# One core, a two-block transformer stack: GpSimd's tensor work outside the FFNs moves to VectorE, and a head pair's value products run in one go

## The chip, the core and the metric

The kernel runs on one core of a Trainium2 chip. The core has a matrix engine (TensorE, PE in the rows; PEld is its weight load), a vector engine (VectorE, DVE), an engine for activation functions (ScalarE, ACT), a general engine (GpSimd, POOL) and SyncE (SP), which here only issues DMAs. Each engine works through a list of its own in a fixed order, and the lists meet at semaphores. TensorE writes to PSUM, a memory of 8 banks of 128 partitions x 2 KB; everything else lies in SBUF. The metric is device time in microseconds (us), lower is better.

## The reference, cut to what matters

Two different blocks follow each other on 512 tokens of width 1024. The first holds an S5 state space branch, a gated branch, cross attention to 256 memory tokens and a SwiGLU FFN; the second is run twice (two layers), each with four branches and an FFN with a short convolution:

```python
def first_block(x, mem, ...):
    n = rms_norm(h, mix_norm_g[i])
    proj = n @ w_in[i]
    ya = s5_branch(xa, ...)                 # bidirectional scan, 512 wide
    yb = sgu_branch(zu, zv, ...)            # 8 heads, chunks of 128
    h = h + (gate_a * (ya @ w_proj_a[i]) + gate_b * (yb @ w_proj_b[i])) @ w_out[i]
    h = h + memory_cross_attention(rms_norm(h, xattn_norm_g[i]), memn, ...)
    h = h + swiglu(rms_norm(h, ffn_norm_g[i]), w_gate[i], w_up[i], w_down[i])

def second_block(x, ...):
    for l in range(DEPTH_2):                # two layers
        z = rmsnorm(x, attn_norm[l]) @ w_in[l]
        yA = forgetting_attention(...)      # 8 heads of 64, causal, a decay per key
        yB = dsa_attention(...)             # 8 heads, top-256 keys chosen by an indexer
        yC = retention(...) ; yD = sliding_window_gqa(...)   # window 128, sinks
        branch = jnp.einsum('bsnc,ncd->bsnd', jnp.stack([yA, yB, yC, yD], 2), w_branch[l])
        x = x + jnp.sum(jax.nn.sigmoid(gates) * branch, axis=2) @ w_out[l]
        a, b = jnp.split(causal_dwconv(rmsnorm(x, ffn_norm[l]) @ w_up[l], ...), 2, axis=-1)
        x = x + (jax.nn.silu(a) * b) @ w_down[l]

def forgetting_attention(...):              # the shape that yB and yD share
        p = jax.nn.softmax(jnp.where(causal, logits, neg), axis=-1)
        return jnp.einsum('bhqs,bshd->bqhd', p.astype(v.dtype), v)
```

## The kernel before, in words

Activations lie transposed, feature on partition, as 8 tiles of 128x512. A product in full precision is made of three products of rounded parts: every operand is split into a rounded part `hi` and a rest `lo`, and `mm3` (L186 to L191) multiplies hi by hi (L189), hi by lo (L190) and lo by hi (L191). So each weight tile of 128x1024 comes by DMA into `raw` (2 buffers), ScalarE rounds it into `hi` (`split`, L167), and `lo = raw - hi` is a subtraction through the helper `tt` (L112). `hi` and `lo` have 3 buffers each; a weight tile feeds 24 matmuls of 512 columns. Who subtracts is set by `weights` (L177 to L185) with a counter: `lo_every` is 1000 in the mixing parts (`mix1`, `mix2`), where GpSimd does nearly all, 2 from `memory_k` to the end of the cross attention, where GpSimd does every second one, and 0 in the FFNs, where VectorE does all. Some other elementwise work is written for GpSimd: six of eight adds of a norm's sums of squares (`square_sum`), the sine product of `rope`, the sum over branches (`merged`), two products of `retain`, one of four output products of `finish`, and the products of the FFNs.

Attention in the second block runs for pairs of heads. `attend` (L952) is a generator that the projections around it advance a step at a time (`pump`): for each of the four chunks of 128 queries the scores (into a PSUM bank `sc`), their maximum (L968), Exp, the reciprocal and the scaling (L982); one chunk later two sets of transposes (L995), ScalarE's copy of them to `probT` (L998, 3 buffers of 512), and the value products (L1003): one head fills rows 0 to 63 of the only `pv` bank, the other rows 64 to 127, so each is a matmul with 64 columns of weights, where the other matmuls around it have 128. There are 8 pairs a layer whose chunks see 1, 2, 3 and 4 key blocks (20 value products) and 4 with 1, 2, 2 and 2 (14). A value product is in float32 and shows as two matmuls in the trace. `select` finds the 256 best keys with 16 rounds of MAX8 (L1127) and MATCH_REPLACE8 (L1128) for three chunks of queries, 48 of each a layer, on VectorE.

The order on each engine is not written out: the code gives a program order, the tile framework puts every instruction into its engine's list by priority and by its own model of durations, and it gives out buffers (`g` has 52 slots of 128x512). `high_priority` pulls instructions ahead, and `manual_schedule` keeps those of one engine together in the order that is written.

## Time and profile before

| | us |
|---|---|
| median of 3 runs (3116.22 to 3117.85) | 3117.04 |
| the profiled execution, its own time | 3118.62 |
| span of the profiled execution | 3116.7 |
| TensorE busy | 3031.5 |
| VectorE busy | 1884.2 |
| ScalarE busy | 1352.9 |
| GpSimd busy | 974.6 |

The stages of the span, by when their weights are fetched: 0 to 480 us the first mixing part, to 605 the cross attention, to 962 the first FFN, 962 to 1605 and 2045 to 2715 the mixing parts of the two layers, 1605 to 2045 and 2715 to the end their FFNs. A matmul's record lasts longer than the time until the next may start, so a busy TensorE is read together with the distances between starts. In the chain of work that ended last, each step is followed back to what released it.

### The profile page before, as it was taken

What the parts mean: (1) busy time and instruction counts of PE and PEld (TensorE: products, weight loads), DVE (VectorE), ACT (ScalarE), POOL (GpSimd) and SP (SyncE); (2) the same over time, 40 slices, a digit from 0 to 9 for tenths busy, and PEclk for the clock granted to TensorE, in tenths of its full rate; (3) what the DMA queues carried; (4) which work ended last, traced back from release to release, by engine and by line L of the source; (5) the groups of instructions that cost most, each with busy time, mean ns of one, the idle gap of its engine ahead of it and who ended that gap; (6) DMA issues with size and microseconds to landing.
All of it is one profiled execution on the core that took longest, in us unless ns stands there. A gap on an engine that the chain in (4) does not pass through costs nothing.

```text
span 3116.7 us, 39233 instructions
## 1 busy us (share of the span) xinstructions
PE 3031.5 (97%) x14922; PEld 2481.6 (80%) x14922; DVE 1884.2 (60%) x3423; ACT 1352.9 (43%) x2278; POOL 974.6 (31%) x594
## 2 busy tenths in 40 slices
PE   8998999999999999999999999999999999999998
PEld 6877878888887777778888888888677778888887
DVE  7899454454455596455456665548845455465575
ACT  5523343332224475646334333356555452343343
POOL 3234243210014442345454000054333445610011
PEclk9999999999999999999999999999999999999999
DMA  5223343223333321222223323242211222333332
GB/s 161 75 80 95 102 146 105 95 88 102 101 90 94 102 75 55 68 78 82 78 88 122 95 91 105 81 133 78 68 55 61 92 75 78 122 96 100 95 96 80
DMA packets 98075, 287.10 MB, mean 92 GB/s; under 512 B 11984, under 2 KB 20432, under 8 KB 97888
## 3 DMA queue, kind: packets, MB, share of 16 engines
q1 hardware_dynamic: 97888, 284.61, 29.6%
q8 instruction: 117, 1.92, 0.3%
q14 instruction: 70, 0.57, 0.1%
HBM read 274.64 MB, written 9.93 MB: 91 GB/s over the span
## 4 chain that ended last, share of the span: by engine, by line
PE 82%; DVE 11%; ACT 2%; DMA 2%; issue 2%; POOL 1%; SPq 0%; DVEq 0%; ACTq 0%; POOLq 0%
PE psmm L189 24%; PE psmm L190 24%; PE psmm L191 24%; DVE tmp L112 3%; PE pspv L1003 2%; DVE g L112 2%; PE pssc L995 1%; DVE g L1128 1%; DVE m L1127 1%; PE pssc L1093 1%; DVE tmp L1217 1%; PE pssc L1094 1%; DVE s5t L112 0%; PE pspv L791 0%; PE pssc L759 0%
## 5 line engine op out<-in xcount | busy, mean ns | idle before, releaser
L191 PE MATMUL psmm<-g,lo 128*128 128x512 f32 (+1 forms) x3456 | 1346.8, 390 | 4.0 <-POOL lo L112 4.0
L190 PE MATMUL psmm<-g,hi 128*128 128x512 f32 (+1 forms) x3456 | 1348.2, 390 | 1.5 <-DVE g L171 1.5
L189 PE MATMUL psmm<-g,hi 128*128 128x512 f32 (+1 forms) x3456 | 1346.4, 392 | 2.3 <-ACT g L167 1.3
L167 ACT CAST hi<-raw 128x1024 fp32r<-128x1024 f32 (+3 forms) x506 | 507.6, 1005 | 1035.3 <-PE psmm L190 748.5
L112 POOL TENSOR_TENSOR lo<-raw,hi 128x1024 fp32r<-128x1024 f32 (+1 forms) x259 | 630.6, 2436 | 1008.8 <-ACT hi L167 849.2
L191 PEld LDWEIGHTS psmm<-g,lo 128*128 128x128 f32 x3456 | 650.3, 188 | 138.4 <-POOL lo L112 5.3
L189 PEld LDWEIGHTS psmm<-g,hi 128*128 128x128 f32 x3456 | 650.2, 188 | 135.4 <-ACT hi L167 3.1
L190 PEld LDWEIGHTS psmm<-g,hi 128*128 128x128 f32 x3456 | 650.8, 188 | 132.3 <-issue 2.6
L112 POOL TENSOR_TENSOR tmp<-tmp,tmp 128x512 f32<-128x512 f32 (+1 forms) x121 | 166.8, 1381 | 1019.1 <-DVE tmp L1419 570.7
L112 DVE TENSOR_TENSOR lo<-raw,hi 128x1024 fp32r<-128x1024 f32 (+2 forms) x247 | 298.0, 1207 | 90.7 <-ACT hi L167 90.6
L112 DVE TENSOR_TENSOR tmp<-psmm,g 128x512 f32<-128x512 f32 x236 | 161.4, 688 | 295.9 <-PE psmm L191 248.3
L189 PE MATMUL psmm<-hi,g 128*128 128x512 f32 (+1 forms) x384 | 144.5, 384 | 16.4 <-ACT g L124 11.1
L1445 DVE SCALAR_TENSOR_TENSOR g<-psmm,g 128x512 f32<-128x512 f32 x88 | 60.7, 690 | 151.7 <-PE psmm L191 151.7
L124 ACT ACTIVATE prob<-prob,nmx 128x128 f32<-128x128 f32 (+2 forms) x192 | 102.5, 535 | 106.7 <-DVE nmx L968 105.9
L190 PE MATMUL psmm<-lo,g 128*128 128x512 f32 (+1 forms) x384 | 146.5, 384 | 2.4 <-POOL lo L112 2.4
L191 PE MATMUL psmm<-hi,g 128*128 128x512 f32 (+1 forms) x384 | 145.2, 382 | 0.0
L112 DVE TENSOR_TENSOR g<-tmp,g 64x512 fp32r<-64x512 f32 (+1 forms) x162 | 130.5, 806 | 14.1 <-ACT g L167 11.0
L124 ACT ACTIVATE tmp<-tmp 128x512 f32<-128x512 f32 (+1 forms) x138 | 84.2, 613 | 111.4 <-DVE tmp L112 98.5
L1419 DVE SCALAR_TENSOR_TENSOR tmp<-tmp,vec,tmp 128x511 f32<-128x511 f32 (+1 forms) x176 | 131.0, 746 | 2.0 <-ACT tmp L124 0.6
L998 ACT COPY probT<-pssc 128x128 f32<-128x128 f32 (+2 forms) x192 | 69.8, 397 | 88.3 <-PE pssc L995 83.3
L189 PEld LDWEIGHTS psmm<-hi,g 128*128 128x128 f32 x384 | 75.1, 196 | 29.2 <-ACT g L124 11.1
L982 DVE TENSOR_SCALAR prob<-prob,sm 128x128 f32<-128x128 f32 (+2 forms) x192 | 93.2, 527 | 2.5
(276 smaller groups left out, 3117.6 us busy)
## 6 DMA issues: line engine op xcount, KB each, us to landing
raw<-w_up SPq DMA_DIRECT2D x110, 512.0 KB, 3.5
raw<-w_gates SPq DMA_DIRECT2D x64, 512.0 KB, 3.5
raw<-w_down SPq DMA_DIRECT2D x72, 384.0 KB, 3.1
raw<-w_rope SPq DMA_DIRECT2D x40, 512.0 KB, 3.6
raw<-w_branch SPq DMA_DIRECT2D x32, 512.0 KB, 3.5
raw<-w_out SPq DMA_DIRECT2D x24, 512.0 KB, 3.6
raw<-w_gate SPq DMA_DIRECT2D x22, 512.0 KB, 3.7
raw<-w_fox SPq DMA_DIRECT2D x16, 512.0 KB, 3.5
```

Source lines behind the costliest of these rows:

```text
L112: (eng or self.nc.vector).tensor_tensor(out, a, b, op)
L124: self.nc.scalar.activation(out, in_, func, **k)
L167: nc.scalar.copy(hi, src)
L189: mm(out, sh, mh, start=start, stop=False)
L190: mm(out, sh, ml, start=False, stop=False)
L191: mm(out, sl, mh, start=False, stop=stop)
L982: nc.vector.tensor_scalar(pt[i][:, :nk], pt[i][:, :nk], sm[:, i:i + 1], None, ALU.mult)
L995: nc.tensor.transpose(tr[:, j * P:(j + 1) * P], pt[i][:, j * P:(j + 1) * P], self.ident)
L998: nc.scalar.copy(ptT[:, :n * P], tr[:, :n * P])
L1003: nc.tensor.matmul(pv[i * 64:(i + 1) * 64, pc * P:(pc + 1) * P], value(i, b), tt[i][:, j * P:(j + 1) * P], start=j == 0, stop=j == n - 1)
L1419: nc.vector.scalar_tensor_tensor(o[:, sh:], u[:, :S - sh], w, o[:, sh:], ALU.mult, ALU.add)
L1445: self.nc.vector.scalar_tensor_tensor(self.x[d], ps, 0.5, self.x[d], ALU.mult, ALU.add)
```

## The change

All GpSimd arithmetic outside the FFNs goes to VectorE: the `lo` subtractions of all weights (with the counter and its four constants gone), the sums of squares, the sine products, the sum over branches, `retain`'s products and the output's. What stays on GpSimd are the FFNs' products, memsets and a few small copies. In `attend` a chunk's transposed probabilities are kept in buffers of their own size until the pair's last chunk; then all value products of the pair are issued together, last chunk first, in a block that is scheduled by hand and with high priority. `g` loses 4 slots.

```diff
-NSLOT = 52
+NSLOT = 48
-LO_MIX1, LO_MEM, LO_MIX2, LO_FFN = 1000, 2, 1000, 0
+NPT = (2, 6, 2, 2)
...
-        self.n_lo += 1
-        pool = self.lo_every and self.n_lo % self.lo_every != 0
-        self.split(hi[:, :width], lo[:, :width], raw[:, :width], eng=self.nc.gpsimd if pool else None)
+        self.split(hi[:, :width], lo[:, :width], raw[:, :width])
...
-            self.add(acc, acc, sq, self.nc.gpsimd if k < KT - 2 else None)
+            self.add(acc, acc, sq)
...
-            self.add(self.merged[d], self.merged[d], t, nc.gpsimd)
+            self.add(self.merged[d], self.merged[d], t)
...
-                    self.mul(o[:, i], self.x[q * 4 + i][:, ts], rb, nc.gpsimd if i == 3 else None)
+                    self.mul(o[:, i], self.x[q * 4 + i][:, ts], rb)
...
-        self.mul(xs, xs, self.sinR, nc.gpsimd)
+        self.mul(xs, xs, self.sinR)
...
-        pv = None
+        done = []
...
-                if pv is None:
-                    pv = self.bank("pv")
...
-                    ptT = self.t(self.ap, [P, S], "probT", bufs=3)
-                    nc.scalar.copy(ptT[:, :n * P], tr[:, :n * P])
+                    ptT = self.t(self.ap, [P, n * P], f"probT{n}", bufs=NPT[n - 1])
+                    nc.scalar.copy(ptT, tr[:, :n * P])
                     tt.append(ptT)
+                done.append((pc, bl, tt))
                 yield
+            pend = nxt
+
+        pv = self.bank("pv")
+        with self.tc.manual_schedule(engines={mybir.EngineType.PE}), self.tc.high_priority():
+            for pc, bl, tt in reversed(done):
                 for j, b in enumerate(bl):
                     for i in range(2):
                         nc.tensor.matmul(pv[i * 64:(i + 1) * 64, pc * P:(pc + 1) * P],
                                          value(i, b), tt[i][:, j * P:(j + 1) * P],
-                                         start=j == 0, stop=j == n - 1)
-                yield
-            pend = nxt
+                                         start=j == 0, stop=j == len(bl) - 1)
+        yield
...
-                    self.mul(qx[:, j], q[j][:, cs], xi[:, j], nc.gpsimd)
+                    self.mul(qx[:, j], q[j][:, cs], xi[:, j])
...
-                    self.mul(Rn, R, gC, nc.gpsimd)
+                    self.mul(Rn, R, gC)
...
-                self.add(self.merged[d], self.merged[d], g, nc.gpsimd)
+                self.add(self.merged[d], self.merged[d], g)
...
-        self.mul(self.cosR, self.cload("cos"), self.rb, nc.gpsimd)
-        self.mul(self.sinR, self.cload("sin"), self.rb, nc.gpsimd)
+        self.mul(self.cosR, self.cload("cos"), self.rb)
+        self.mul(self.sinR, self.cload("sin"), self.rb)
```

The list of TensorE before, in layer 0, where one head pair's chunks 1 to 3 follow each other (`pspv`, L1003 are its value products, `probT` its transposed probabilities, `h` the values of four key blocks; `pssc` of L1081, L1082, L1093 are scores and of L995 transposes of `prob`):

```order
L1081 MATMUL pssc_2034_9699<-g_1868_9005,g_1866_9003 128x512
L1082 MATMUL pssc_2034_9699<-g_1872_9009,g_1870_9007 128x512
L1003 MATMUL pspv_2011_9620<-probT_2027_9684,h_1641_8124 64x128
L1081 MATMUL pssc_2035_9703<-g_1869_9006,g_1867_9004 128x512
L1082 MATMUL pssc_2035_9703<-g_1873_9010,g_1871_9008 128x512
L1003 MATMUL pspv_2011_9620<-probT_2029_9689,h_1641_8124 64x128
L1003 MATMUL pspv_2011_9620<-probT_2027_9684,h_1642_8125 64x128
L1003 MATMUL pspv_2011_9620<-probT_2029_9689,h_1642_8125 64x128
L995 MATMUL pssc_2036_9712<-idn_2_71,prob_2020_9664 128x128 x3
L995 MATMUL pssc_2038_9718<-idn_2_71,prob_2021_9665 128x128 x3
L1003 MATMUL pspv_2011_9620<-probT_2037_9716,h_1641_8124 64x128
```

The pair's value products stand one to six at a time, with scores and transposes of 128 columns between them. The list of TensorE now, for the first head pair of layer 0 (the value products are L1000 here, and `probT4` holds chunk 3):

```order
L187 MATMUL psmm_2027_9648<-g_1572_7762,hi_2029_9651 128x512
L188 MATMUL psmm_2027_9648<-g_1571_7761,lo_2030_9652 128x512
L1000 MATMUL pspv_1804_8758<-probT4_1791_8700,h_1641_8124 64x128
L1000 MATMUL pspv_1804_8758<-probT4_1793_8707,h_1641_8124 64x128
L1000 MATMUL pspv_1804_8758<-probT4_1791_8700,h_1642_8125 64x128
L1000 MATMUL pspv_1804_8758<-probT4_1793_8707,h_1642_8125 64x128
L1000 MATMUL pspv_1804_8758<-probT4_1791_8700,h_1643_8126 64x128
L1000 MATMUL pspv_1804_8758<-probT4_1793_8707,h_1643_8126 64x128
L1000 MATMUL pspv_1804_8758<-probT4_1791_8700,h_1644_8127 64x128
L1000 MATMUL pspv_1804_8758<-probT4_1793_8707,h_1644_8127 64x128
L1000 MATMUL pspv_1804_8758<-probT3_1787_8687,h_1641_8124 64x128
L1000 MATMUL pspv_1804_8758<-probT3_1789_8693,h_1641_8124 64x128
```

The run goes on through chunks 2, 1 and 0 to 20 value products without another instruction between them. Over the whole program the value products stand in 139 groups before and in 34 now: 8 of 20, 8 of 19, 6 of 14, 2 of 13 and 10 single ones that stand a few instructions ahead of their run.

The list of VectorE before, in layer 0, amid the selection (`m8` and the `g` beside it are the 8 largest scores and the scores of one chunk; L968 are the maxima of attention scores):

```order
L112 TENSOR_TENSOR tmp_1957_9380<-tmp_1957_9380,tmp_1958_9381 128x512
L1127 MAX m8_1848_8937<-g_1715_8444 128x8
L1127 MAX m8_1874_9029<-g_1662_8254 128x8
L1127 MAX m8_1875_9032<-g_1693_8359 128x8
L112 TENSOR_TENSOR h_1598_7878<-psmm_1971_9426,g_1585_7807 128x512
L1128 MATCH_REPLACE g_1715_8444<-m8_1848_8937,g_1715_8444 128x512
L1128 MATCH_REPLACE g_1662_8254<-m8_1874_9029,g_1662_8254 128x256
L1128 MATCH_REPLACE g_1693_8359<-m8_1875_9032,g_1693_8359 128x384
L968 ISA prob_1828_8863,nmx_1829_8864<-pssc_1832_8870,cst2_1589_7837 128x128
L968 ISA nmx_1829_8864 128x1
L1127 MAX m8_1876_9035<-g_1715_8444 128x8
```

No `lo` stands between the first and the last of the layer's 48 MAX8 (they are in the list of GpSimd). The list of VectorE now, at a place of the same stretch (MAX8 is L1123, MATCH_REPLACE L1124, the helper of L112 is L111):

```order
L1123 MAX m8_1883_9061<-g_1662_8254 128x8
L1123 MAX m8_1884_9064<-g_1693_8359 128x8
L111 TENSOR_TENSOR lo_2078_9873<-raw_2076_9870,hi_2077_9872 128x1024
L111 TENSOR_TENSOR g_1819_8838<-tmp_1817_8834,g_1819_8838 64x512
L1124 MATCH_REPLACE g_1715_8444<-m8_1858_8965,g_1715_8444 128x512
L111 TENSOR_TENSOR g_1826_8845<-tmp_1818_8835,g_1822_8841 64x512
L1124 MATCH_REPLACE g_1662_8254<-m8_1883_9061,g_1662_8254 128x256
L1124 MATCH_REPLACE g_1693_8359<-m8_1884_9064,g_1693_8359 128x384
L111 TENSOR_TENSOR h_1601_7881<-psmm_2042_9735,g_1585_7807 128x512
L973 RECIPROCAL sm_1810_8789<-sm_1810_8789 128x2
L973 RECIPROCAL sm_1836_8885<-sm_1836_8885 128x2
```

Between the first and the last MAX8 of layer 0 the list of VectorE now has 235 instructions where it had 205: 19 `lo` of 1024 columns, 4 sine products of 512 columns and 7 others more. The list of TensorE has 459 matmuls of 512 columns in float32r between the same two marks where it had 394. Layer 1 reads alike (236 for 202, 19 `lo`).

## Rows read from the trace of the kernel before

**Rows 1.** The page: busy time by engine, then the chain that ended last, by engine.

```profile
PE 3031.5 (97%) x14922; PEld 2481.6 (80%) x14922; DVE 1884.2 (60%) x3423; ACT 1352.9 (43%) x2278; POOL 974.6 (31%) x594
...
PE 82%; DVE 11%; ACT 2%; DMA 2%; issue 2%; POOL 1%; SPq 0%; DVEq 0%; ACTq 0%; POOLq 0%
```

**Rows 2.** Busy time by engine in seven stretches: stretch, its us, busy us (instructions).

```profile
0.00:310.00 310.00, 279.11 (x1417) 229.95 (x1418) 265.59 (x568) 128.60 (x181) 116.19 (x89) 0.98 0.35 103
605.00:962.00 357.00, 357.00 (x1579) 295.35 (x1578) 177.41 (x199) 103.05 (x128) 36.84 (x25) 1.00 0.32 95
962.00:1058.00 96.00, 85.93 (x406) 71.84 (x405) 59.12 (x71) 53.08 (x82) 53.90 (x29) 0.93 0.36 113
1058.00:1177.00 119.00, 114.34 (x544) 90.26 (x543) 104.40 (x252) 76.74 (x140) 52.17 (x31) 1.00 0.23 74
1177.00:1605.00 428.00, 425.38 (x2295) 337.47 (x2294) 227.62 (x573) 210.59 (x458) 180.26 (x101) 1.00 0.23 73
2108.00:2230.00 122.00, 115.77 (x552) 91.72 (x550) 110.06 (x250) 77.74 (x140) 52.34 (x31) 1.00 0.24 76
2230.00:2715.00 485.00, 480.99 (x2537) 383.31 (x2536) 254.38 (x599) 232.38 (x487) 218.68 (x120) 1.00 0.25 79
```

**Rows 3.** TensorE in order of time: start us, us, one value product between matmuls.

```profile
1389.23 0.39 PE L189 MATMUL psmm<-hi,g 128*128 128x512 f32 x1
1389.55 0.43 PE L1003 MATMUL pspv<-probT,msc 128*64 128x128 f32 x2
1389.91 0.39 PE L1093 MATMUL pssc<-g,g 128*128 128x256 f32 x1
```

**Rows 4.** TensorE in order of time: plain matmuls, then eight value products in a run.

```profile
1248.10 0.39 PE L190 MATMUL psmm<-g,hi 128*128 128x512 f32 x1
1248.32 0.39 PE L191 MATMUL psmm<-g,lo 128*128 128x512 f32 x1
1248.64 1.09 PE L1003 MATMUL pspv<-probT,msc 128*64 128x128 f32 x16
1249.66 0.33 PE L1093 MATMUL pssc<-g,g 128*128 128x128 f32 x1
```

**Rows 5.** Line 1003, the value products: forms, with min/median/max ns of one.

```profile
L1003 PE MATMUL pspv<-probT,msc x544: 272/273/325, 1227.5 to 2571.7; 128*64 128x128 f32 x182
L1003 PE MATMUL pspv<-probT,h x320: 272/273/325, 1113.2 to 2278.5; 128*64 128x128 f32 x160
```

**Rows 6.** Groups of instructions, GpSimd: shapes and count | busy us, mean ns.

```profile
L112 POOL TENSOR_TENSOR lo<-raw,hi 128x1024 fp32r<-128x1024 f32 x255 | 622.8, 2444 | 990.8 <-ACT hi L167 831.2 <-PE pssc L995 53.4 <-issue 27.8
```

**Rows 7.** The same view, VectorE.

```profile
L112 DVE TENSOR_TENSOR lo<-raw,hi 128x1024 fp32r<-128x1024 f32 x159 | 216.0, 1358 | 90.6 <-ACT hi L167 90.6
L112 DVE TENSOR_TENSOR tmp<-psmm,g 128x512 f32<-128x512 f32 x236 | 161.4, 688 | 295.9 <-PE psmm L191 248.3 <-ACT tmp L925 24.3 <-ACT g L266 8.9
L112 DVE TENSOR_TENSOR s5h<-s5h,s5t 128x64 f32<-128x64 f32 x63 | 30.9, 491 | 1.8
```

**Rows 8.** GpSimd, then VectorE, in order of time around one `lo`.

```profile
1496.23 2.41 POOL L112 TENSOR_TENSOR lo<-raw,hi 128x1024 fp32r<-128x1024 f32 x1 [3.30 <-ACT hi L167]
...
1497.03 1.63 DVE L112 TENSOR_TENSOR es<-vec,nmx 128x2 f32<-128x2 f32 x1
1498.93 0.16 DVE L112 TENSOR_TENSOR sm<-sm,es 128x2 f32<-128x2 f32 x1 [0.27 <-ACT es L124]
```

**Rows 9.** Who TensorE waited for: us in total, times, longest.

```profile
PE pssc L661 <- DVE s5b L654: 4.9, 1, 4.9
PE pspv L379 <- DVE tmp L383: 4.1, 4, 1.3
PE pspv L1003 <- ACT probT L998: 4.1, 8, 0.9
PE psmm L191 <- POOL lo L112: 4.0, 3, 1.7
```

**Rows 10.** The chain in order of time: start us, us; the longest VectorE burst.

```profile
1574.83 8.13 DVE tmp L1217 x21
```

More of the change, by code (lines that the diff above doesn't have):

```diff
@@ L78, in __init__ @@
         self.bg, self.bg2 = [], []
-        self.lo_every, self.n_lo = 0, 0
         pool = lambda name, bufs, **k: ctx.enter_context(tc.tile_pool(name=name, bufs=bufs, **k))
@@ L161, in debug, with split @@
             self.nc.sync.dma_start(self.O[name], ap)
-    def split(self, hi, lo, src, scale=None, eng=None):
+    def split(self, hi, lo, src, scale=None):
         nc = self.nc
@@ L167, in split @@
             nc.scalar.copy(hi, src)
-            self.sub(lo, src, hi.bitcast(F32), eng)
+            self.sub(lo, src, hi.bitcast(F32))
         else:
@@ L303, in mix1 @@
         nc, I = self.nc, self.I
-        self.rate, self.lo_every = 1, LO_MIX1
+        self.rate = 1
         xa_d = self.dram.tile([S, 512], F32, name="xa_d")
@@ L313, in mix1 @@
                 raws[k // 2] = self.raw(I["w_xa"][k // 2], 1024)
-        self.lo_every = 0
         for u in range(4):
@@ L332, in mix1 @@
                              u == 0 and k == 0, u == 3 and k == 1)
-        self.lo_every = LO_MIX1
         for c in range(CHUNKS):
@@ L410, in mix1 @@
                 rm = fin()
-        self.lo_every = LO_MEM
         self.memory_k(m, rm[0])
@@ L800, in ffn1 @@
         nc, I = self.nc, self.I
-        self.lo_every = LO_FFN
         x, fin = self.rms_prep(self.x, "g_ffn", S)
@@ L1303, in mix2 @@
         nc, ap, I = self.nc, self.ap, self.I
-        self.rate, self.lo_every = 1, LO_MIX2
+        self.rate = 1
         wr = I["w_rope"][l]
@@ L1400, in ffn2 @@
         cw, cb = self.vec(f"cw{l}"), self.vec(f"cb{l}")
-        self.lo_every = LO_FFN
         j = 0
```

## The prediction

> **What bounds the kernel now.** I read the page first. TensorE is busy 3031.5 of 3116.7 us, and the chain that ended last lies on it for 82% and on VectorE for 11% [rows 1]. A busy share is an average, so the busy time by stretch comes next [rows 2]: in the first FFN TensorE is busy for all of 357 us, and in the later parts of the two mixing stages (1177 to 1605, 2230 to 2715) for over 99%. The first 310 us (279 of 310) and the head of layer 0 (86 of 96) are the loose ones. In three stretches VectorE is nearly full: the first 310 us (266 busy) and the two selections (104 of 119, 110 of 122). GpSimd is full nowhere. So a gain has to come from time on TensorE that does no work although it counts as busy, or from waits in the loose stretches; a loss would come through VectorE where it is full. For the first, the order of time on TensorE shows distances between starts [rows 3, 4]; for the second, the groups on GpSimd and VectorE and a place where the two meet [rows 6 to 8]; who TensorE waited for closes the list [rows 9].
>
> **The value products.** A plain matmul of 512 columns starts 0.22 us after the one before [rows 4]; over all pairs of them the median is 0.227. A value product after such a matmul starts 0.32 us after it, and the next full-width matmul starts 0.36 us after a lone product [rows 3]. Beyond the plain 0.227 the lone product costs 0.32 + 0.36 - 0.227 = 0.45 us. Eight in a run take 0.32 + 1.02 = 1.34 us, less 0.227 = 1.11 [rows 4]. The two heads of a pair write different halves of the array and start within 6 ns of each other when they alternate, so eight products are eight steps (four pairs, two records each) where the lone one is two: (1.11 - 0.45) / 6 = 0.11 us a step, and 0.45 - 0.22 = 0.23 us are fixed, paid for the change from 128 to 64 columns and back. A lone product takes the time of two.
>
> There are 864 records, 432 products [rows 5], and before they stand in 139 groups. By size: 67 of one or two products at 0.45, 40 of three or four at 0.68, 8 of five at 0.89, 8 of six at 1.2, 16 of seven or eight at 1.11: 30 + 27 + 7 + 10 + 18 = 92 us; a count of the single groups in the trace gives 93.9, and I use that. Now there are 34: 16 of 19 or 20 products, 20 steps each, 0.23 + 2.20 = 2.43; 8 of 13 or 14, 1.77; 10 lone ones, 0.45: 39 + 14 + 4.5 = 57.6. The gain is 36 us. Fourteen of the old groups lie in the selections, where VectorE may set the pace; I leave their share, 4 us, out. **-32 us** (bounds -36 and -15; the lower end is in the rivals). The other 32 lie where TensorE is busy over 99% [rows 2], so they are on the path. What is late next there: the runs need the last chunk's transposes copied by ScalarE, which is busy about half of those stretches [rows 2].
>
> **GpSimd's work on VectorE.** GpSimd made 255 `lo` of 1024 columns at 2.44 us [rows 6]. VectorE's own take 1.36 in the mean [rows 7], and 1.225 is the median of the 133 that have no GpSimd instruction beside them. With some 130 products and sums of 512 columns at 0.69 (the mean of a VectorE product of that size [rows 7]), 24 small ones and the rest, VectorE takes on 414 us of instructions. Against this stands what GpSimd costs it now. An instruction of 2 elements lasted 1.63 us and ended with the `lo` on GpSimd (1497.03 + 1.63 = 1498.66, 1496.23 + 2.41 = 1498.64), and its like right after, with GpSimd idle, 0.16 [rows 8]. An add of 64 columns in the S5 scan has a mean of 0.49 [rows 7] where its median alone is 0.225. Products that read PSUM show no such stretching: 0.688 [rows 7] for all, 0.691 alone. Taking each VectorE instruction against the median of its own kind without GpSimd beside it, 312 us of VectorE's time are such waiting, 43 of them in FFN stretches, where GpSimd stays. So VectorE ends near 1884 + 414 - 269 = 2029 us, 65% of the span. From 1177 to 1605 it gets 94 more and 49 back on 228 of 428: that is hidden behind TensorE, and free. Where VectorE is full it has to be counted.
>
> *Selections.* In layer 0 the list of VectorE between the first and the last MAX8 gains 19 `lo` (23.3 us), 4 sine products (2.7) and 7 small ones (2.6), 28.6 in all, and gets 10 back: 104.4 + 28.6 - 10 = 123 us busy, and with today's 14.6 us of waits 138. The list of TensorE between the same marks takes 65 matmuls (14.8) and 14 transposes (1.5) more, so 119 + 16 = 135 would be no loss. Between 123 and 138 against 135, twice: -20 to +6; the waits stay where they are in part, and I take **+2 us** for both.
>
> *First 310 us.* VectorE takes over 39 `lo` and 10 sums, 53 us, and gets 75 back. TensorE's waits on VectorE and GpSimd in the first 480 us are 18.5 us, the largest among them 4.9 on a small S5 copy and 4.1 on the gate's sum [rows 9]. A third of these is my estimate, **-6 us**, between -18 and +10 (an S5 chain that now shares its queue with the `lo`).
>
> *Heads of the layers.* From 962 to 1058 TensorE idles 10 us [rows 2] behind norms whose adds of 512 columns GpSimd did and VectorE now does at 0.69 [rows 7]; VectorE takes on 24 us there and gets 23 back. **-4 us** with the smaller head of layer 1, between -8 and +2.
>
> *Queues.* A `lo` now waits behind whatever VectorE is at; behind it waits TensorE's third matmul of each step. With three buffers of `hi` and `lo`, and 24 x 0.227 = 5.4 us of matmuls a weight tile, a `lo` may come some 5 us late before TensorE sees it. The output's one product and the four slots less of `g` I put at 0, between -1 and +3: nothing but TensorE's look-ahead hangs on the slots, and its list shows the selections reaching further ahead than before.
>
> **Sum.** The profiled execution took 3118.62 us: -32 + 2 - 6 - 4 gives 3078.6. That execution lies 1.6 above the median of the runs, so I predict **3077 us**, 40 less.
>
> **A rule that speaks against it.** The rows just named show VectorE waiting out GpSimd. The Trainium skill, Perfetto Trace Analysis, section Optimizing Scalar/DVE Operations, says that when the vector engine is saturated, moving some of its work to ScalarE or even GpSimd may make sense, and adds that between these two it might not help, since they share a read port. By its first half this change goes the wrong way in the three full stretches, and the sum would be that of rival 1, 3119; the trace bears out its second half, 1.63 us for 0.16 [rows 8].
>
> **The rivals.**
> 1. *VectorE fills up.* If its instructions do not get shorter, the selections need 104.4 + 28.6 + 14.6 = 148 us against 135, +12 each, and the first stretch 266 + 53 = 319 of 310, +10: -32 + 24 + 10 and no gain at the heads, 3118.6 + 2 - 1.6 = 3119: no change. For it: VectorE's 104 of 119 us in the selection [rows 2]. Against it: the stretching in rows 7 and 8, which cannot outlive its cause.
> 2. *Late `lo`, the slower end.* If VectorE falls more than one weight tile behind, each of the 39 + 19 + 19 = 77 `lo` in the full stretches can hold TensorE for the instruction ahead of it, 0.69 us: +53, so 3077 + 53 = 3130; with half of the selections of rival 1, 24 / 2 = 12 more, 3142. I price it at 3136, between them. It decides from a backlog of 5.4 us on; one burst in the trace is longer, 8.1 us [rows 10], with few `lo` beside it. Against it: GpSimd's `lo` of 2.44 us cost TensorE's third matmuls only 4.0 us in three waits [rows 9].
> 3. *The runs wait.* Each of 24 runs may wait for its last copy. Such waits now are 4.1 us in 8, the longest 0.9 [rows 9]; 24 x 0.9 = 22 us takes two thirds of the gain: 3099. It is also what the change gives if the runs do not hold together on the chip as in the list.
> 4. *More comes back.* If VectorE's shorter instructions remove all 18.5 us of waits in the first 480 us and the selections end 8 us earlier, 3077 - 12.5 - 8 = 3057.
>
> **How the numbers follow.** Forecast 0.62 (3064 to 3090), rival 1 0.07, rival 2 0.06, rival 3 0.13, rival 4 0.12. The range takes in the forecast, rivals 3 and 4 and leaves out 0.13: 3055 to 3105. A difference of 0.2% (6.2 us) is about what a measurement tells from none: faster 0.62 + 0.13 + 0.12 = 0.87, same 0.07, slower 0.06.
>
> **What would show it.** The runs: line 1000 with 0.11 us a step and 105 groups fewer, so 1177 to 1605 shortens by 15 us and 2230 to 2715 likewise. VectorE: `lo` at 1.23, the 2-element adds at 0.16, total near 2030. The selections (first to last MAX8): 135 us, with 459 matmuls in them. Waits of TensorE on `lo` near 0. Wrong would be: selections of 145 us or more (rival 1), TensorE waiting on `lo` in VectorE's name by tens of us (rival 2), line 1000 waiting for `probT4` by a microsecond each (rival 3).

## The result and the profile after

The changed kernel takes 3062.94 us (median of 4 runs, 3062.15 to 3063.27) beside 3116.89 us for the kernel before (4 runs): a ratio of 0.9826 (0.9809 to 0.9843), 54 us less. I had predicted 3077, 40 less, with a range of 3055 to 3105. The direction and the range held; where the time came from did not, as the marks below show.

The page of the changed kernel, busy time by engine and the chain that ended last (beside [rows 1]); its profiled execution took 3062.15 us:

```profile
PE 2985.7 (98%) x14922; PEld 2486.8 (81%) x14922; DVE 1983.2 (65%) x3869; ACT 1353.1 (44%) x2276; POOL 116.6 (4%) x148
...
PE 89%; DVE 7%; ACT 2%; DMA 1%; issue 1%; SPq 0%; DVEq 0%; ACTq 0%
```

TensorE is busy 46 us less with the same 14922 matmuls. VectorE is busy 99 us more, where the forecast had 145. That is not a smaller load: the forecast added up lengths of records, and busy time counts records that overlap only once. Added up in the same way, VectorE's records went from 2035 to 2175 us, 140 more.

To see where, I use three marks that both programs pass in the same order: the first product of the gate in each of the three FFNs (the span from the first to the last is 283.7 us in the first FFN and 286.4 or 286.3 in the others, in both kernels, so nothing happened inside them). One line before, then after; each row gives the first and the last start:

```profile
L816 DVE SCALAR_TENSOR_TENSOR tmp<-tmp,tmp x22: 679/684/692, 639.6 to 923.3; 128x512 f32<-128x512 f32 x22
L1424 DVE SCALAR_TENSOR_TENSOR tmp<-tmp,tmp x22: 676/684/692, 1706.9 to 1993.2; 128x512 f32<-128x512 f32 x22
L1424 DVE SCALAR_TENSOR_TENSOR tmp<-tmp,tmp x22: 680/684/686, 2761.4 to 3047.8; 128x512 f32<-128x512 f32 x22
```

```profile
L809 DVE SCALAR_TENSOR_TENSOR tmp<-tmp,tmp x22: 679/685/692, 610.7 to 894.4; 128x512 f32<-128x512 f32 x22
L1419 DVE SCALAR_TENSOR_TENSOR tmp<-tmp,tmp x22: 678/684/687, 1664.9 to 1951.3; 128x512 f32<-128x512 f32 x22
L1419 DVE SCALAR_TENSOR_TENSOR tmp<-tmp,tmp x22: 680/685/687, 2706.2 to 2992.5; 128x512 f32<-128x512 f32 x22
```

The first FFN begins 28.9 us earlier; layer 0 (from the first mark to the second) takes 1054.2 instead of 1067.3, 13.1 less; layer 1 takes 1041.3 instead of 1054.5, 13.2 less. So more than half came from the first block, to which the forecast gave 6, and 26 from the two layers, to which it gave 34.

Busy time in stretches of the changed kernel (columns as in [rows 2]: stretch, its us, then busy us and instructions of TensorE, its weight load, VectorE, ScalarE and GpSimd, then TensorE's granted clock):

```profile
0.00:282.00 282.00, 271.09 (x1418) 227.59 (x1419) 234.85 (x612) 125.23 (x175) 12.08 (x40) 1.00 0.37 111
934.00:1018.00 84.00, 81.22 (x407) 68.82 (x406) 59.22 (x99) 52.78 (x82) 3.60 (x8) 0.98 0.40 131
1017.00:1148.00 131.00, 125.80 (x595) 102.35 (x594) 120.41 (x282) 80.69 (x146) 2.08 (x4) 0.99 0.24 77
1150.00:1190.00 40.00, 30.97 (x209) 25.18 (x210) 23.95 (x77) 24.05 (x65) 0.00 (x0) 0.83 0.04 14
```

The first 1417 matmuls took 310 us before, and 1418 take 282 now. The head of layer 0, 406 matmuls before and 407 now, shrank from 96 to 84 us. The selection holds 595 matmuls in 131 us where it held 544 in 119: the same pace. And right behind it is a stretch that the forecast did not have: 40 us in which TensorE is busy for 31 and is granted 0.83 of its clock.

Who TensorE waited for (us in total, times, longest; beside [rows 9]):

```profile
PE pssc L986 <- DVE prob L975: 23.1, 10, 4.3
...
PE psmm L188 <- DVE lo L111: 3.5, 4, 0.9
...
PE pspv L1000 <- ACT probT L989: 0.7, 2, 0.3
```

The late `lo` that rival 2 feared cost 3.5 us. The runs' own wait for their last copy, which rival 3 priced at 22 us, is 0.7 us. But the transposes of the probabilities (L986) now wait 23.1 us for VectorE to scale them (L975).

### The profile page after: what moved, and what is told of

Same layout as the page of the kernel before. It is cut to its first block, busy times and chain, and to the rows that moved or that the text cites. A ratio compares the mean times of both kernels' runs of the same rounds, so it can differ in the third digit from the quotient of the medians.

```text
span 3060.3 us, 38946 instructions
## 1 busy us (share of the span) xinstructions
PE 2985.7 (98%) x14922; PEld 2486.8 (81%) x14922; DVE 1983.2 (65%) x3869; ACT 1353.1 (44%) x2276; POOL 116.6 (4%) x148
## 4 chain that ended last, share of the span: by engine, by line
PE 89%; DVE 7%; ACT 2%; DMA 1%; issue 1%; SPq 0%; DVEq 0%; ACTq 0%
PE psmm L186 26%; PE psmm L188 26%; PE psmm L187 26%; PE pspv L1000 2%; PE pssc L986 1%; DVE g L111 1%; DVE lo L111 1%; DVE g L1124 1%; DVE m L1123 1%; DVE tmp L111 1%; DVE prob L961 1%; PE pssc L1089 1%; PE pssc L1090 0%; PE pspv L785 0%; PE pssc L753 0%
## 5 line engine op out<-in xcount | busy, mean ns | idle before, releaser
L111 DVE TENSOR_TENSOR lo<-raw,hi 128x1024 fp32r<-128x1024 f32 (+3 forms) x506 | 610.7, 1207 | 215.7 <-ACT hi L166 214.2
L111 DVE TENSOR_TENSOR tmp<-psmm,g 128x512 f32<-128x512 f32 x236 | 161.8, 689 | 294.2 <-PE psmm L188 274.4
L186 PE MATMUL psmm<-hi,g 128*128 128x512 f32 (+1 forms) x384 | 142.7, 380 | 13.5 <-ACT g L123 10.8
L111 POOL TENSOR_TENSOR tmp<-tmp,tmp 128x512 f32<-128x512 f32 x66 | 89.7, 1360 | 1535.2 <-DVE tmp L1414 979.4
L111 DVE TENSOR_TENSOR g<-tmp,g 64x512 fp32r<-64x512 f32 (+2 forms) x166 | 113.4, 684 | 18.1 <-ACT g L166 11.0
L986 PE MATMUL pssc<-idn,prob 128*128 128x128 f32 x432 | 71.2, 286 | 24.1 <-DVE prob L975 23.1
L186 PEld LDWEIGHTS psmm<-hi,g 128*128 128x128 f32 x384 | 73.7, 192 | 25.6 <-ACT g L123 10.8
L918 ACT COPY tmp<-psmm 32x512 f32<-32x512 f32 x160 | 92.5, 578 | 2.4
```

Source lines behind the costliest of these rows:

```text
L111: (eng or self.nc.vector).tensor_tensor(out, a, b, op)
L186: mm(out, sh, mh, start=start, stop=False)
L918: nc.scalar.copy(xs[k * 32:k * 32 + 32], bk[(k ^ 1) * 32:(k ^ 1) * 32 + 32])
L986: nc.tensor.transpose(tr[:, j * P:(j + 1) * P], pt[i][:, j * P:(j + 1) * P], self.ident)
```

## The experiments

In the table each kernel's marks are read on the same two lines as above: by how much the first FFN begins earlier (-) or later than in the kernel before, and by how much each layer is shorter (-) or longer. The median of before, measured beside each batch, was 3117.85 for e1 to e4, 3117.2 for e5 to e8 and 3116.8 for e9 to e12.

| kernel | median us | ratio to before (95%) | first FFN | layer 0 | layer 1 |
|---|---|---|---|---|---|
| changed | 3062.9 | 0.9826 (0.9809-0.9843) | -28.9 | -13.1 | -13.2 |
| e1 runs only | 3140.4 | 1.0073 (1.0058-1.0088) | +0.4 | +11.9 | +7.2 |
| e2 move only | 3072.0 | 0.9856 (0.9840-0.9873) | -27.7 | -10.7 | -7.4 |
| e3 move, first block | 3094.9 | 0.9924 (0.9909-0.9939) | -26.3 | +4.5 | -2.4 |
| e4 lo twice | 3124.5 | 1.0021 (1.0012-1.0030) | +33.4 | -12.7 | -11.3 |
| e5 norm adds | 3114.4 | 0.9992 (0.9982-1.0002) | -4.6 | +1.9 | -0.2 |
| e6 2 steps | 3049.8 | 0.9783 (0.9769-0.9798) | -28.6 | -21.8 | -17.2 |
| e7 scores first | 3068.5 | 0.9841 (0.9826-0.9856) | -30.1 | -11.1 | -6.9 |
| e8 one more step | 3059.7 | 0.9816 (0.9801-0.9830) | -32.3 | -13.4 | -13.3 |
| e9 move only, 2 steps | 3073.5 | 0.9858 (0.9842-0.9874) | -27.1 | -7.5 | -7.7 |
| e10 lead | 3048.1 | 0.9781 (0.9767-0.9796) | -31.3 | -20.6 | -17.7 |
| e11 head by head | 3093.0 | 0.9924 (0.9909-0.9939) | -31.1 | +2.3 | +7.2 |
| e12 lo in selection | 3042.5 | 0.9762 (0.9747-0.9776) | -28.4 | -21.6 | -19.7 |

### The two parts apart: e1 and e2

e1 puts the new `attend` (with NSLOT 48 and NPT) into the kernel before; e2 puts the old one (with NSLOT 52) into the changed kernel.

```diff
 # e1, against the kernel before
-NSLOT = 52
+NSLOT = 48
+NPT = (2, 6, 2, 2)
...
+                done.append((pc, bl, tt))
...
+            for pc, bl, tt in reversed(done):
```

> The kernel before with the new attend alone (value products in runs, buffers by size, 48 slots of g); GpSimd keeps all its work. Theory: a value product's group costs 0.23 us plus 0.109 us a step, so 105 groups fewer give back 32 to 36 us wherever GpSimd's work is done, and nothing else moves: 3117 - 33 = 3084 us (3079 to 3090), with the waits of TensorE in the selections as before (about 4 us each layer). Rival: the 10 us a layer that the changed kernel lost to waits of the transposes on the scaled probabilities come from the runs, which leave nothing but one pair's softmax to work on: then this kernel has them too, 3084 + 20 = 3104 us.

> The changed kernel with the attend of before (value products chunk by chunk, 52 slots): only GpSimd's work is moved to VectorE. Theory: the first 605 us give back 29 us, the heads of the layers 12 and 1, and VectorE's 19 further lo in each selection cost 10 us a layer: 3117 - 42 + 20 = 3095 us (3088 to 3102). Rival (the waits in the selections belong to the runs): 3117 - 42 = 3075 us. By my prediction's own terms (+2 - 6 - 4) it would be 3109 us.

The runs alone made the kernel 22 us slower, worse than the rival of e1, and the move alone made it 46 us faster, near the rival of e2 (3075). The four slots less of `g` and the new `probT` buffers go with the runs in both kernels and were not tried apart. The waits of TensorE in e1 and then in the kernel before, the spans and mean granted clocks of the two, and the same 100 us of each by windows:

```profile
PE pssc L994 <- DVE prob L983: 31.3, 21, 3.0
PE pssc L994 <- DVE nmx L969: 10.8, 5, 3.0
```

```profile
PE pssc L995 <- DVE prob L982: 6.0, 5, 2.2
...
PE pssc L995 <- DVE nmx L968: 2.8, 4, 1.7
```

```profile
core 0: 3137.4 us, clock 0.982
```

```profile
core 0: 3116.7 us, clock 0.991
```

```profile
1150.00:1250.00 100.00, 86.12 (x465) 70.37 (x464) 75.16 (x181) 60.76 (x137) 23.78 (x11) 0.90 0.15 48
```

```profile
1150.00:1250.00 100.00, 95.65 (x550) 73.01 (x549) 70.21 (x188) 56.97 (x135) 26.39 (x11) 1.00 0.18 55
```

The transposes wait 42.1 us in 26 places (31.3 on the scaling, 10.8 on the maximum); in the kernel before it was 8.8 us in 9. Around such waits TensorE is granted its lower level, 1.2 GHz, for a while (0.90 in the mean of these 100 us of e1, 1.00 in those of before). Over the span the mean of 0.982 leaves out 0.018 x 3137 = 56 us, where the kernel before, with a mean of 0.991, leaves out 28. The account: -36 for the groups (the forecast's own price), +33 for the waits, +28 for the clock, -4 for the waits on `probT` that are gone: +21. The span grew by 20.7.

The waits of e2 show the other side, with the transposes' waits where they were, and its mean clock:

```profile
PE pssc L987 <- DVE prob L974: 7.7, 3, 4.3
```

```profile
core 0: 3068.9 us, clock 0.995
```

### What is late, seen in the changed kernel

TensorE, then VectorE, then ScalarE, in order of time, in the stretch behind the first selection (start us, us, what, count, and in brackets the idle time ahead):

```profile
1162.29 1.03 PE L986 MATMUL pssc<-idn,prob 128*128 128x128 f32 x6
1167.57 1.97 PE L986 MATMUL pssc<-idn,prob 128*128 128x128 f32 x8 [4.25 <-DVE prob L975]
...
1171.56 3.19 PE L1000 MATMUL pspv<-probT,h 128*64 128x128 f32 x38
```

```profile
1163.24 0.08 DVE L961 DVE_READ_ACCUMULATOR2_ANT nmx<- 128x1 f32 x1
1163.35 2.84 DVE L111 TENSOR_TENSOR g<-tmp,g 64x512 fp32r<-64x512 f32 x4
1166.82 0.17 DVE L973 RECIPROCAL sm<-sm 128x2 f32<-128x2 f32 x1 [0.63 <-ACT prob L123]
1167.02 0.88 DVE L975 TENSOR_SCALAR prob<-prob,sm 128x512 f32<-128x512 f32 x2
```

```profile
1161.83 2.55 ACT L929 CAST g<-tmp 64x512 fp32r<-64x512 f32 x4
1164.40 0.48 ACT L989 COPY probT<-pssc 128x384 f32<-128x384 f32 x1
1164.90 0.72 ACT L123 ACTIVATE prob<-prob,nmx 128x512 f32<-128x512 f32 x1
...
1165.62 0.46 ACT L989 COPY probT<-pssc 128x384 f32<-128x384 f32 x1
1165.98 0.72 ACT L123 ACTIVATE prob<-prob,nmx 128x512 f32<-128x512 f32 x1
```

The last scores of the chunk end near 1162.3. The way from there through the maximum, the exponential, the reciprocal and the scaling takes until 1167.5, five microseconds, and TensorE's list holds six transposes of 0.11 us for that time. It idles 4.25 us, and the run of 19 products behind it begins at the lower clock (0.53 granted from 1166.0 to 1172.8): 38 records in 3.19 us, where 40 take 2.40 at full clock (below). VectorE is named because its scaling is the last step, but the longest stay is on ScalarE: both maxima are read by 1163.3, and the two exponentials begin at 1164.90 and 1165.98, behind four casts and two copies. So ScalarE's order made this wait, too; another order was not tried.

In the list of the kernel before, 1.1 us of value products of earlier chunks and 1.4 us of a projection stood in this place besides; in e2 it was 0.5 us of value products alone, and there the transposes did not wait. Counting TensorE's work in the lists between a head's last score of a chunk and the first transpose of it, with the trace's distances (0.227 us for 512 columns, 0.119 for 256, 0.109 for 128), 18 of the 192 sets of transposes have less than 4 us of it in the kernel before, 24 in e2, 40 in e1 and 53 in the changed kernel. So the theory became: the runs save what they promise, and the order that comes with them takes away what covered the softmax.

What went is for the smaller part the value products themselves. The 29 sets that fall below 4 us from e2 to the changed kernel lose 3.8 us of projections each in the mean and 0.1 us of value products (in some a run of the pair before stands there now): the order of the list changed around them. And less cover is not all of it. In the changed kernel every wait of the transposes lies at a set with less than 4 us of work, but in e1 31 of the 42 us lie at sets with 6 to 21 us, where the way to the scaled probabilities took 7 to 24 us. What made it so long beside GpSimd's work was not tried.

### Testing the cover: e6, e9, e8, e7, e10

e6 changes one number of the changed kernel, e9 the same number of e2; e8 adds a step; e10 is e6 with other leads; e7 is e6 with `with self.tc.high_priority():` around the scores and around the softmax in `attend`.

```diff
 # e6 and e9, in mix2
-        self.rate = 4
+        self.rate = 2
 # e8, in attend
                 done.append((pc, bl, tt))
                 yield
+                yield
 # e10, beside rate = 2
-LEAD = (4, 3, 3, 3)
+LEAD = (4, 4, 3, 4)
```

> The changed kernel with one number changed: in the first half of a layer's mixing part a projection advances the attention by 2 steps instead of 4. In TensorE's list 40 instead of 53 of the 192 sets of transposes then stand less than 4 us of TensorE's work behind their scores, the runs stay whole (34 groups). Theory (TensorE waits because the runs took away what lay between a chunk's scores and its transposes): the 23 us of waits of the transposes on the scaled probabilities fall to 12 to 17, and the time to 3048 to 3058 us. Rival (VectorE is full in the selections, whatever the order): waits as before, 3060 us or more.

> The kernel with the move alone (value products chunk by chunk as before) and 2 steps a projection instead of 4 in the first half of a layer's mixing part, the number that made the changed kernel 13 us faster. Its list of TensorE has 27 sets of transposes less than 4 us behind their scores where it had 24. Theory (2 steps help only because they give the runs' transposes back what lay between them and their scores): no gain, 3068 to 3078 us beside 3072. Rival (2 steps are better for any order of the value products): about 3060 us, and the runs are worth no more than before.

One row each, the transposes' wait on the scaling in e6 and in e9:

```profile
PE pssc L986 <- DVE prob L975: 15.5, 8, 3.4
```

```profile
PE pssc L987 <- DVE prob L974: 6.9, 6, 4.4
```

e6 gave 3049.8 us and 15.5 us of waits, both inside what the theory said; with the value products spread as before, the same number gave nothing (3073.5 beside 3072.0). So the 13 us belong to the order with runs. Compared like with like the runs are worth 3073.5 - 3049.8 = 24 us with 2 steps, 9 us with 4 (3072.0 - 3062.9) and a loss of 22 beside GpSimd's work.

> The changed kernel with one more step for each chunk of the attention, which the attend of before has (its value products were a step of their own): 47 instead of 53 sets of transposes stand less than 4 us behind their scores, 36 groups of value products. Theory: a part of the waits goes, 5 to 10 us: 3053 to 3060 us. Rival (the steps have nothing to do with it): 3063 us, with the 23 us of waits as they are.

> The changed kernel with 2 steps (3050 us) and with one more gate projection ahead of two of the four branch products, so that other work stands between the last pairs' softmax steps: 34 instead of 40 sets of transposes less than 4 us behind their scores, 36 groups. Theory: 3 to 8 us less, 3042 to 3047 us. Rival (what is left of the waits is VectorE's): 3048 to 3052 us.

e8 took 3 us off, at 3059.7 inside its range, with 19.4 us of waits, but it proves little: its layers are as long as the changed kernel's (it waits 4 us less, and its mean clock of 0.988 leaves out 9 us more), and its gain lies ahead of the first FFN, where the lists of the two kernels are the same. (In e6 and e10 they are the same there too, and the marks of these four lie between -28.6 and -32.3: so far apart can single executions be.) e10 came to 3048.1, which is the rival's side: the waits went from 15.5 to 13.4 us and the time by less than can be told apart.

> The same with the scores and the softmax of the attention scheduled at high priority: 30 of the 192 sets of transposes stand less than 4 us behind their scores, but scores now cut the runs into 93 groups, 59 more, each at 0.23 us: +13.6 us. Theory: the waits of the transposes fall to 6 to 12 us, which gives 11 to 17 us and the half clock that goes with them, about 5: 3063 + 14 - 19 = 3058 us (3050 to 3065). If the groups cost nothing beyond their steps: 3044 us. If the waits stay: 3077 us.

e7 had 11.0 us of such waits, as expected, and still took 3068.5, slower than its range. By the distances between starts its 93 groups cost 79 us, the 34 of e6 62: 17 more where 59 x 0.23 = 14 were counted. TensorE is busy 25 us more (3009.2 instead of 2983.8); where the other 8 come from I did not separate. Two thirds of the 93 begin behind a score of 256 columns. Here, cover bought by cutting the runs cost more than it gave.

Among these kernels, which all have the runs and VectorE's `lo`, the waits on the scaling follow the count of short sets: 53, 47, 40, 34 and 30 sets (changed, e8, e6, e10, e7) and 23.1, 19.4, 15.5, 13.4 and 11.0 us.

### The price of a step: e11

```diff
-            for pc, bl, tt in reversed(done):
-                for j, b in enumerate(bl):
-                    for i in range(2):
+            for i in range(2):
+                for pc, bl, tt in reversed(done):
+                    for j, b in enumerate(bl):
```

> The changed kernel, in which a run goes through the products of the first head and then through those of the second, so that neighbours no longer write different halves of the array. Still 34 groups. Theory (two heads that alternate share a step of 0.109 us, the term by which the prediction priced a run): 432 products take 432 more steps, +47 us: 3063 + 47 = 3110 us, less up to 13 for the transposes, of which 35 instead of 53 sets stand less than 4 us behind their scores: 3095 to 3112 us. Rival (a step is a product's own time, whatever its neighbour): 3050 to 3065 us.

A run of 20 products in the changed kernel, and 10 products of one head in e11, each with the instruction behind it, the run also with the one ahead:

```profile
1216.48 0.39 PE L186 MATMUL psmm<-g,hi 128*128 128x512 f32 x1
1216.80 2.40 PE L1000 MATMUL pspv<-probT,msc 128*64 128x128 f32 x40
1219.14 0.33 PE L1089 MATMUL pssc<-g,g 128*128 128x128 f32 x1
```

```profile
1148.15 2.40 PE L1000 MATMUL pspv<-probT,h 128*64 128x128 f32 x20 [0.34 <-ACT probT L989]
1150.48 0.33 PE L1077 MATMUL pssc<-g,g 128*128 128x128 f32 x1
```

Forty records of alternating heads and twenty of one head take the same 2.40 us: two neighbours in different halves of the array share their time. e11 is 30 us slower than the changed kernel, 2 us below the range that I gave: not every pair was parted (a run that goes from the first head to the second still alternates there), and 18 sets of transposes had more cover. The Trainium skill, TensorEngine Tiling (Array Packing), section Tiling Modes, says that different tiles of the array can execute their loads and matmuls in parallel, and that a change of the tiling mode drains the engine. The traces agree with the first. For the second they show a price, 0.23 us for the change there and back [rows 3, 4], and not what the engine does in that time.

### The first block: e3 and e4

e3 is the kernel before with LO_MIX1 and LO_MEM at 0 and the first block's sums on VectorE. e4 is the changed kernel with one subtraction more for every weight of the first mixing part, whose result nobody reads:

```diff
+        if self.twice:
+            two = self.t(self.mp, [P, 1024], "two", bufs=1)
+            self.sub(two[:, :width], raw[:, :width], hi[:, :width].bitcast(F32), self.nc.gpsimd)
...
+        self.twice = True
...
+        self.twice = False
```

> The kernel before with GpSimd's work moved to VectorE in the first block alone (lo of the first mixing part, the cross attention and its memory, the sums of squares of these norms, the sum over branches); the two layers keep theirs and their value products. Theory from the two traces: the first FFN begins 29 us earlier, everything behind it is as before: 3088 us (3084 to 3092). By the prediction's term for this stretch (-6, at most -18): 3111 us (3099 at the least).

> The changed kernel, in which GpSimd subtracts every lo of the first mixing part a second time, into a scratch buffer that nobody reads (39 subtractions of about 2.4 us); the result that TensorE uses still comes from VectorE. Theory (the 25 us of the first 310 us come from VectorE no longer waiting out GpSimd): the stretch of VectorE's instructions comes back, some 50 to 75 us of them, and with it 15 to 25 us of time: 3078 to 3088 us. Rival (they come from lo being ready sooner and from fewer hand-overs between engines, which this kernel keeps): 3063 to 3068 us.

e3's first FFN begins 26.3 us earlier: the first block's gain stands by itself, and it is not 6 us. The time, 3094.9, is 3 us above the range of the theory: of the gain 2 us are lost again in the layers, whose own code e3 leaves alone. e4 is more than was expected of either theory: all of the gain is gone and 33 us more. Groups of instructions in its first 337 us, one of GpSimd's and two of VectorE's; then the stretch with 1418 matmuls:

```profile
L112 POOL TENSOR_TENSOR two<-raw,hi 128x1024 f32<-128x1024 f32 x39 | 112.0, 2873 | 195.5 <-ACT hi L167 179.9 <-issue 9.1 <-DMA raw<-w_zu 5.8
L112 DVE TENSOR_TENSOR lo<-raw,hi 128x1024 fp32r<-128x1024 f32 x42 | 61.3, 1460 | 5.7 <-ACT hi L167 5.3 <-issue 0.2
L112 DVE TENSOR_TENSOR s5h<-s5h,s5t 128x64 f32<-128x64 f32 x63 | 20.4, 324 | 1.4
```

```profile
0.00:337.50 337.50, 288.93 (x1418) 235.52 (x1419) 309.16 (x604) 124.62 (x175) 123.34 (x79) 0.95 0.31 93
```

The changed kernel's values for the two groups of VectorE, in its first 253 us:

```profile
L111 DVE TENSOR_TENSOR lo<-raw,hi 128x1024 fp32r<-128x1024 f32 x39 | 47.6, 1221 | 7.8 <-ACT hi L166 7.3
L111 DVE TENSOR_TENSOR s5h<-s5h,s5t 128x64 f32<-128x64 f32 x63 | 14.0, 223 | 1.4
```

Nobody waits for `two`, and yet VectorE is busy 309 us instead of 235 for the same work, and the stretch takes 337.5 us instead of 282: +74 in, +55 out. The second reading also holds `raw` and `hi` longer, and TensorE waited 15.7 us for `lo` in e4 (3.5 in the changed kernel); how much of the 55 that is was not tried. In the kernel before VectorE is busy for 266 us of the stretch, and e3 and e4 together speak for VectorE as the engine that set the pace there.

### The heads of the layers: e5

```diff
-            self.add(acc, acc, sq, self.nc.gpsimd if k < KT - 2 else None)
+            self.add(acc, acc, sq)
```

> The kernel before with one part of the move alone: the sums of squares of all norms are added on VectorE, everything else stays on GpSimd. Theory (the heads of the layers are bound by the chain of a norm's adds, one behind the other: 10 adds of 1.61 us on GpSimd become 0.69 us, 9 us): the head of layer 0 ends 9 to 12 us earlier than in the kernel before, the time is 3103 to 3109 us. Rival (the heads gain because lo and the adds no longer share GpSimd's queue, so that both have to leave): under 4 us, 3113 us or more.

The head of layer 0 in e5 and the stretch of the selection behind it:

```profile
958.00:1047.00 89.00, 82.61 (x408) 69.46 (x407) 63.29 (x89) 52.65 (x82) 39.16 (x21) 0.96 0.39 125
1047.00:1175.00 128.00, 116.91 (x555) 91.50 (x554) 118.39 (x258) 79.65 (x145) 50.41 (x29) 0.99 0.21 66
```

408 matmuls in 89 us, 7 less than before, so the adds are more than half of the head's 12 us; but the selection behind it, with GpSimd's `lo` still beside it, takes 128 us for 555 matmuls where it took 119 for 544, and layer 0 ends up 1.9 us longer. The time, 3114.4, cannot be told from before. The theory on the head's price was about right, and its range for the kernel was wrong; the time is the rival's, whose reason does not fit the head. What the head gained was lost again in the next stretch.

### A faster version: e12

e12 is e6 with a switch that is on while `select` runs: `split` then gives `lo` to GpSimd.

```diff
         self.bg2.append(sel)
+        self.pool_lo = True
...
                 self.drain(sel)
+                self.pool_lo = False
```

> The changed kernel with 2 steps (3050 us), in which GpSimd makes the lo of the weights that are projected during the selections, 13 a layer, and VectorE all others. Theory (VectorE bounds the selections, and its lo there are what they cost): VectorE loses 13 x 1.22 = 16 us a layer and gets 4 to 7 us of stretching, so each selection ends about 9 us earlier, of which half reaches the end: 3036 to 3044 us. Rival (the stretching and a later lo take all of it back): 3047 to 3056 us.

3042.5 us is the lowest median of all, 20 us below the changed kernel. Against e6 the ratios overlap (0.9747 to 0.9776 and 0.9769 to 0.9798), its four runs spread over 9 us, and its profiled execution, the longest of them, has a span 2 us shorter than e6's. The time lies inside the theory's range, but not by its way: from the first to the last MAX8 the selections take 137.7 and 139.4 us, in e6 137.8 and 140.3, so they do not end 9 us earlier. That e12 and e6 beat the changed kernel is shown; that e12 beats e6, and by what, is not.

## Why the prediction was right, and where it was not

**The price of the runs: right.** A run of 20 starts 0.32 us behind a matmul of 512 columns and ends with the next start 2.34 later (1216.80 to 1219.14): less 0.227 that is the 2.43 us of the forecast. There are 34 runs and lone products, as counted. Of the 16 longest, 12 cost 2.3 to 2.4 us; the other four begin at the lower clock and cost 3.2 to 3.8.

**What the runs give: the step that failed.** Of -32 the changed kernel got 9 (e2 to changed). The forecast asked "what is late next there" and answered with the copies to `probT`; that wait is 0.7 us. It did not ask what TensorE's list would have between a chunk's scores and its transposes once the products were gone from there and the rest had moved up. The new order opened 15 us of waits on the scaled probabilities (7.7 to 23.1) and some 11 us of clock (the mean is 0.995 over 3068.9 us in e2, 0.991 over 3060.3 in the changed kernel). e6 and e9 show that it is the order: one number gives 13 us with the runs and nothing without them. Rival 3 had the size nearly right, 22 us of 32, and the place wrong.

**The first block: a term of the wrong kind.** -6 became -29. The forecast saw that VectorE takes on 53 us there and gets 75 back, net -22, and that it is busy 266 of 310; then it took a third of TensorE's 18.5 us of waits. Where one engine is nearly full, its net work is the term: -22 is what the row says and -28 is what came (310 to 282), with VectorE busy 31 us less (266 to 235). Even rival 4 gave it no more than the 18.5 us of waits.

**The heads.** -4 became -12 in layer 0. The forecast took -4 out of TensorE's 10 us of idle time; that the adds follow one another, ten of them in the head and each some 0.9 us shorter, it named and did not price. e5 bears out 7 of the 12; where the other 5 come from was not tried.

**The selections.** +2 was about right: the pace is the same, from the first to the last MAX8 of layer 0 it takes 132 us where the forecast said 135, and with the move alone both layers get shorter, by 10.7 and 7.4. (The lower bound of that term, -20, is a slip: 123 against 135, twice, is -24.) Rivals 1 and 2 did not happen.

**The sum.** The first block was put 23 us too low, the heads and selections 16 (the layers of e2 are 18 us shorter where 2 were forecast), the runs 23 too high: 23 + 16 - 23 = 16, and the span came out 56 us shorter where 40 were forecast. So the range held by luck: errors of opposite sign took each other's part.

## What to carry to other kernels

Before work is moved out of a place, look at which wait it covers there: a saving on TensorE that is certain by itself came out as -24, -9 or +22 us, by what stood between scores and transposes and by how long the way between them was. In a stretch where one engine is nearly full, that engine's net change was nearer to the gain here than a share of the waits on it. And when two parts of a change share a resource, time each alone: here one part alone was a loss.

## What the runs showed of the hardware

The clock made waits dearer than their length: in e1 33 us of added waits came with 28 us of lower clock, about as much again. It is no fixed price: from the changed kernel to e6 the waits on the scaling fell by 8 us and the mean clock stayed within 0.001 (0.991 and 0.992), and e8 had 4 us less of them at a lower mean, 0.988.

GpSimd's subtractions whose result nobody reads came with 55 us more in a stretch of 282 (e4), and instructions with two inputs in SBUF were longer on both engines: 2.87 us for GpSimd's subtraction and 1.46 for VectorE's, where it is 2.41 in [rows 8] and 1.22 in the changed kernel. The Trainium skill, SBUF — State Buffer, section SBUF: two separate sides, says that these instructions and GpSimd's take a shared port pair in turn, each for its whole length; the traces agree, on both engines.
